# Moving three pieces of work in a two-layer hybrid decoder trunk on one core

## The chip, the core and the metric

The kernel runs on one core of a Trainium2 chip. A core has TensorE (PE; its weight loads are shown as PEld), VectorE (DVE), ScalarE (ACT), GpSimd (POOL) and SyncE (SP, which here only starts transfers). The metric is the device time of one execution in microseconds (us).

## What is computed

The reference is a trunk of two layers over one sequence of 256 tokens with 1024 features, all in float32. Each layer is a feed-forward block, a token mixer and a second feed-forward block; each of the three has its own norm, and a conditioning vector `c` gives every one of them a shift, a scale and a gate by a product with `w_ada`.

```python
for l in range(DEPTH):                                   # 2
    mod = (silu(c) @ w_ada[l] + b_ada[l]).reshape(B, 3, 3, D_MODEL)
    # norm_mod(h, j) = rms(h) * g_norm[l, j] * (1 + mod[:, j, 1]) + mod[:, j, 0];  gate(j) = 1 + mod[:, j, 2]
    x = x + 0.5 * gate(0) * swiglu(norm_mod(x, 0), w_ffn_up[l, 0], w_ffn_down[l, 0])   # hidden width 2816
    x = x + gate(1) * mixer(norm_mod(x, 1), ...)
    x = x + 0.5 * gate(2) * swiglu(norm_mod(x, 2), w_ffn_up[l, 1], w_ffn_down[l, 1])
# mixer: one input projection feeds a gated linear recurrence (512 wide), a stick-breaking attention
# and a forgetting attention (256 each); each result is RMS-normed over its own features, the three are
# concatenated, scaled and multiplied by w_out.
```

## The kernel before

**Precision and weight units.** Every product of a weight runs as three passes (high x high, high x low, low x high), so each operand exists as a high part and a low part. Weights come in units of 128 x 1024 (512 KB). `unit` starts the transfer into one of 6 `raw` buffers (queue of SP), and `split` makes the high part `H` on ACT (line 246) and the low part `L` on DVE (line 247). H and L have 11 buffers each.

**Conditioning dots.** A step of `ada_step` moves one 512 KB unit of `w_ada` through the same `raw` buffers and the same queue of SP and multiplies it with `c` on DVE with an accumulated sum: `ada_ss` (line 292, shift and scale) and `ada_gate` (line 317, gate). 128 steps stand in one list in the order in which the norms and gates need them. `ADA_FFN` and `ADA_MIX` (line 69) say how many are taken off the list after each chunk of a feed-forward block and after each projection of the mixer of a layer; `ada_until` takes what is left when a norm or a residual needs it. In the mixer of layer 0 there are nine projections and ten steps (`proj` takes one each, `proj_w` of the stick-breaking group one for each of its two halves); in layer 1 there are none. After the mixer of layer 0 eleven more are forced by the norm of the next block.

**Feed-forward block.** `ffn` walks 11 chunks of 256 hidden features. The first block of layer 0 has a path of its own (`pre`); the other three take the `else` list of line 568. There `u` (`up`) is the 24 products of one chunk for one half `t` of the tokens (128 tokens), followed by silu on ACT and a multiply on DVE; `r` (`tr`) transposes that product on PE into a PSUM tile `tg` of the pool `PT` and splits it (ACT line 535, DVE line 536); `d` (`down`) is its 12 products with the down weights; `w` (`up_w`) does a half chunk for all tokens, which needs no transposes. The block begins while the norm of the second half of the tokens is still being made: `flush` puts that half's transposes (`norm_out`, tile `tp`, line 418, also pool `PT`, which has two buffers) behind a product inside `u(1, 0)`, and `u(0, 1)` is the first that reads the result (`hTh`, `hTl`).

**Mixer.** The projections come in the order LG, LX (gate and input of the recurrence, one call per half of the tokens, LG 0, LX 0, LG 1, LX 1), FX, SB, VV. As in the feed-forward block, the norm of the second half of the tokens is finished inside LX 0. The recurrence ends in `hs` (scan on DVE, times the transposed gate `tl`). `group` norms a result over its features: a square on ACT, adds on DVE, one product with ones (`mo`, line 801, which sums over partitions), logarithm and exponential on ACT, a multiply on DVE. For `hs` this is written ahead of the VV projections. The attention products that follow are placed with `behind(...)`, an edge that only says after which instruction of the same engine one may be issued.

**Who sets the order.** The code is written in program order, and the framework's planner orders each engine's queue ahead of time: among the instructions whose inputs its own clock takes to be ready, the one written first goes first, and `high_priority` moves an instruction ahead in that choice. On the chip each queue then runs in that fixed order.

Of the kernel before, what the change touches and what calls it, by code (L numbers as in the profile page):

```python
# [9 lines left out]
F32 = mybir.dt.float32  # L10
# [14 lines left out]
SEQ = 256  # L25
# [4 lines left out]
LX, LG, SB, FX, VV = range(5)  # L30
# [14 lines left out]
def weight_units():  # L45
    keys = []
    for l in range(DEPTH):
        for s in range(2):
            for j in range(NCH):
                keys += [("up", l, s, j, h) for h in range(4)] + [("dn", l, s, j, i) for i in range(2)]  # L50
            if s == 0:
                for g in GROUP_ORDER:
                    keys += [("in", l, g, h) for h in range(4)]
                keys += [("out", l, m) for m in range(KT)]
    return {k: i for i, k in enumerate(keys)}
# [10 lines left out]

N_PRE = 4
K_T = (4, 2, 4)
ADA_FFN, ADA_MIX = ((5, 4), (5, 3), (5, 1), (5, 2)), (1, 0)
W_UNITS = weight_units()  # L70
A_UNITS = ada_units()

# [22 lines left out]
def trunk_kernel(ctx: ExitStack, tc: tile.TileContext, x, c, wst, ada, par, cst, row, wg, out):  # L95
# [14 lines left out]
    def W4(shape, dt=F32, name="w4"):  # L110
        return w4.tile(shape, dt, tag="w4", name=name)

    def W2(shape, dt=F32, name="w2"):
        return w2.tile(shape, dt, tag="w2", name=name)
# [4 lines left out]
    def PA(shape, name):  # L119
        return psa.tile(shape, F32, tag="a", name=name)  # L120
# [4 lines left out]
    def PT(shape, name):  # L125
        return pst.tile(shape, F32, tag="t", name=name)

    V, A, T, S = nc.vector, nc.scalar, nc.tensor, nc.sync
# [67 lines left out]
    ones_r, ntri_r, nones_r = (const.tile([128, 128], F32R, name=n + "_r") for n in ("ones", "ntri", "nones"))  # L196
# [53 lines left out]
    def unit(key):  # L250
        if key not in live:
            raw = rawp.tile([128, 1024], F32, tag="raw", name="raw")
            S.dma_start(out=raw, in_=wst[W_UNITS[key]])
            live[key] = split(raw)
        return live[key]
# [6 lines left out]
    def over_features(o, t, w, mid=None, by=4):  # L262

        hh, hl = hT[t]
        muls = []
        for k0 in range(0, KT, by):
            for k in range(k0, k0 + by):
                for i, part in enumerate(w(k)):  # L270
                    T.matmul(o, lhsT=hh[:, k, :], rhs=part, start=k == 0 and i == 0, stop=False)  # L271
            for k in range(k0, k0 + by):
                mul = T.matmul(o, lhsT=hl[:, k, :], rhs=w(k)[0], start=False, stop=k == KT - 1)  # L273
                muls.append(mul)
                if mid and mid[0] == k:
                    mid[1](mul)
        return muls
# [62 lines left out]
    def ada_step(n):  # L340
        for _ in range(n):
            if ada_todo:
                f, a = ada_todo[-1]
                if f is ada_gate and a[2] == 0:
                    if not gate_free[a[1] % 2]:
                        return
                    gate_free[a[1] % 2] = False
                ada_todo.pop()
                f(*a)
# [110 lines left out]
    def act(*a, **k):  # L460
        with tc.issue_after(table[-1].ins) if table else nullcontext():
            used.append(A.activation(*a, **k))  # L462
        return used[-1]
# [9 lines left out]
    def ffn(l, s, after, pre={}):  # L473
# [88 lines left out]
        u, w, r, d = up, up_w, tr, down  # L562
        if pre:
            ops = [(w, (0, 0)), (w, (0, 1)), (w, (1, 0)), (w, (1, 1)), (d, (0, 0)), (w, (2, 0)), (d, (0, 1)),
                   (w, (2, 1)), (d, (1, 0)), (w, (3, 0)), (d, (1, 1)), (w, (3, 1)), (w, (4, 0)), (d, (2, 0)),
                   (d, (2, 1)), (w, (4, 1)), (d, (3, 0)), (d, (3, 1))]
        else:
            ops = [(u, (0, 0)), (u, (1, 0)), (r, (0, 0)), (u, (0, 1)), (r, (1, 0)), (d, (0, 0)), (u, (1, 1)),
                   (r, (0, 1)), (d, (1, 0)), (w, (2, 0)), (r, (1, 1)), (d, (0, 1)), (w, (2, 1)), (d, (1, 1))]
        a, b = NCH - 2, NCH - 1  # L570
        for j in range(5 if pre else 3, a):
# [13 lines left out]
    def mixer(l, after):  # L585
# [7 lines left out]
        muls = {}  # L593

        def proj(g, t):
            o = PA([128, 512], name="pj")

            def w(k):
                q = slice((k % 2) * 512, (k % 2 + 1) * 512)
                return [part[:, q] for part in unit(("in", l, g, k // 2))]  # L600

            muls[g, t] = over_features(o, t, w, (K_T[2], flush) if (g, t) == (LX, 0) else None, by=1)
            ada_step(ADA_MIX[l])
            return o

        def proj_w(g, b):
# [16 lines left out]
        def behind(mul):  # L623
            return tc.issue_after(mul.ins)
# [6 lines left out]
        for t in range(NT):  # L631
            act(lgt[:, t], proj(LG, t), AF.Gelu_apprx_tanh)
            tok = W2([128, 512], name="lxt")
            A.copy(tok, proj(LX, t))
            tp = PT([128, 4, 128], name="tx")
            for i in range(4):
                T.transpose(tp[:, i, :], tok[:, i * 128:(i + 1) * 128], ident)
            A.copy(xT[:, :, 3 + t * 128:3 + (t + 1) * 128], tp)


        u = W4([128, 4, SEQ], name="u")
# [28 lines left out]
        qa = [const.tile([128, 8, 66], F32, name=f"qa{t}", tag=f"qa{t}") for t in range(NT)]  # L670
        for t in range(NT):
            o = proj(FX, t)
            if t == 1:
                z4 = SM([128, NT, 4], name="z4")
# [12 lines left out]
            sq = W2([128, 8, HD], name="fsq")  # L687
# [42 lines left out]
        hs = W4([128, 4, SEQ], name="hs")  # L730
# [45 lines left out]
        def split(f0, n, src):  # L776
            for i in range(n):
                g = gm[:, f0 + i:f0 + i + 1]
                yh, yl = hTh[:, :, f0 + i, :], hTl[:, :, f0 + i, :]
                y = src[:, i, :].rearrange("p (t q) -> p t q", t=NT)  # L780
                A.activation(yh, y, AF.Copy, scale=g)
                V.scalar_tensor_tensor(out=yl, in0=y, scalar=g, in1=yh.bitcast(F32),
                                       op0=ALU.mult, op1=ALU.subtract)
# [6 lines left out]
            q = slice(t * 128, (t + 1) * 128)  # L790
            V.tensor_tensor(out=hs[:, :, q], in0=hs[:, :, q], in1=tp, op=ALU.mult)

        def group(y, n, sq, out):

            A.activation(sq, y, AF.Square)
            while n > 1:
                n //= 2
                V.tensor_tensor(out=sq[:, 0:n, :], in0=sq[:, 0:n, :], in1=sq[:, n:2 * n, :], op=ALU.add)
            n = out.shape[1]
            mo = PT([128, SEQ], name="mo")  # L800
            T.matmul(mo, lhsT=ones_r.bitcast(F32), rhs=sq[:, 0, :], start=True, stop=True)
            rl = W2([128, SEQ], name="rl")
            act(rl, mo, AF.Ln, scale=1.0 / (128 * n), bias=eps_t)
            act(rl, rl, AF.Exp, scale=-0.5)
            V.tensor_tensor(out=out, in0=y, in1=rl.unsqueeze(1).to_broadcast([128, n, SEQ]), op=ALU.mult)

        group(hs, 4, W4([128, 4, SEQ], name="lsq"), hs)

        vt = W4([128, 2, 512], name="vt")
        for t in range(NT):  # L810
            A.copy(vt[:, t], proj(VV, t))
        split(0, 4, hs)


# [64 lines left out]

        def normed(f0, y):  # L880
            yn = W2([128, 2, SEQ], name="yn")
            group(y, 2, W2([128, 2, SEQ], name="gsq"), yn)
            split(f0, 2, yn)

        yfx, ysb = (PD([128, 2, SEQ], name=n) for n in ("yfx", "ysb"))
        values(yfx, 256, lambda part, p, e: (pa, pb)[part][:, 2 * p + e, :])
        normed(6, yfx)
        o = {}

# [20 lines left out]
        for m, t in [(m, 0) for m in WO[:4]] + [(m, 1) for m in WO[:1]] + [(m, 0) for m in WO[4:-2]]:  # L910
            mul = w_out(m, t)
            if (m, t) == (WO[1], 0):
                with behind(mul):
                    values(ysb, 0, lambda part, p, e: (wsa, wsb)[part][:, e, p, :])
                normed(4, ysb)
                load_table("silu_and_others")
# [56 lines left out]
    for l in range(DEPTH):  # L973
        ffn(l, 0, norm(l, 1), pre if l == 0 else {})
        mixer(l, norm(l, 2))
        ffn(l, 1, norm(l + 1, 0) if l + 1 < DEPTH else None)
# [94 lines left out]
```

## Time and profile before

| | |
|---|---|
| time, median of 3 runs | 1011.37 us (1008.23 to 1013.19) |
| profiled execution | 1010.85 us, of which the span from first to last instruction is 1009.0 us |
| PE / PEld / DVE / ACT busy | 982.2 / 857.9 / 761.4 / 532.9 us |
| share of the chain that ended last: PE / DVE / ACT | 86% / 7% / 5% |
| mean granted TensorE clock | 0.995 of full |

All times inside the execution are counted from the start of the span. Matmuls overlap in the profile, so the rate of PE is read from the starts of successive products, and lost time from the gaps between them. In the timeline a bracket at the end of a row is idle time of the engine just before the row and what released it.

### The profile page before, as it was taken

The page shows a single profiled execution, that of the slowest core. Times are in us where ns is not written, and L with a number is a line of the kernel's source. Part 1 is how long each engine was busy: PE and PEld are TensorE (multiplying, and loading weights), DVE is VectorE, ACT ScalarE, POOL GpSimd, SP SyncE. Part 2 cuts the span into 40 slices and gives each one's busy share as a digit, 9 for nine tenths or more (in the row PEclk, how much of TensorE's full clock was granted, in tenths as well). Part 3 has the DMA queues.
Part 4 walks back from the last instruction along what each step waited for, and adds up shares of the span by engine and source line. Part 5 has one row for each costly group of instructions (what it writes and reads, how often), then busy time and mean ns, then how long its engine had stood idle before and what let it go on. Part 6 is the DMA issues. An engine that isn't in the chain of part 4 may idle for free.

```text
span 1009.0 us, 15828 instructions
## 1 busy us (share of the span) xinstructions
PE 982.2 (97%) x6054; PEld 857.9 (85%) x6054; DVE 761.4 (75%) x1224; ACT 532.9 (53%) x854; POOL 6.9 (1%) x16
## 2 busy tenths in 40 slices
PE   6999999989999999999999999999999999999998
PEld 4999999867867799999878999997788778999996
DVE  8988888788996988888589888765778588636352
ACT  5373435558775534355465344455678655535340
POOL 0000000000000000000000000000000000000000
PEclk9999999999999999999999999999999999999999
DMA  8999999677382999999449999854542349655511
GB/s 320 352 336 341 350 330 342 237 259 268 127 279 96 318 370 331 343 327 329 171 165 339 361 346 335 310 177 157 189 167 84 105 155 343 241 180 192 185 64 42
DMA packets 69966, 251.26 MB, mean 249 GB/s; under 512 B 8066, under 2 KB 8706, under 8 KB 69891
## 3 DMA queue, kind: packets, MB, share of 16 engines
q1 hardware_dynamic: 68834, 247.09, 69.3%
q0 software_dynamic: 1056, 3.17, 1.0%
q8 instruction: 47, 0.77, 0.3%
q14 instruction: 29, 0.23, 0.1%
HBM read 249.16 MB, written 1.07 MB: 248 GB/s over the span
## 4 chain that ended last, share of the span: by engine, by line
PE 86%; DVE 7%; ACT 5%; issue 1%; DMA 1%; ACTq 0%; DVEq 0%; SPq 0%
PE up L470 38%; PE dn L258 8%; PE dn L260 8%; PE dn L259 8%; PE up L271 6%; PE pj L271 5%; PE up L273 3%; PE pj L273 2%; DVE L L247 2%; PE wo L258 1%; PE wo L259 1%; PE wo L260 1%; ACT hf L426 1%; ACT H L246 1%; DVE raw L292 1%
## 5 line engine op out<-in xcount | busy, mean ns | idle before, releaser
L247 DVE TENSOR_TENSOR L<-raw,H 128x1024 fp32r<-128x1024 f32 x320 | 381.5, 1220 | 79.1 <-ACT H L246 78.0
L246 ACT CAST H<-raw 128x1024 fp32r<-128x1024 f32 x320 | 327.9, 1051 | 114.1 <-DMA raw<-in_wst 61.3
L470 PE MATMUL up<-hTh,H 128*128 128x256 f32 x1088 | 209.9, 280 | 2.4 <-ACT H L246 1.9
L470 PE MATMUL up<-hTl,H 128*128 128x256 f32 x1088 | 210.0, 281 | 0.0
L470 PE MATMUL up<-hTh,L 128*128 128x256 f32 x1088 | 209.3, 280 | 0.0
L470 PEld LDWEIGHTS up<-hTh,H 128*128 128x128 f32 x1088 | 167.5, 188 | 8.8 <-ACT H L246 2.3
L470 PEld LDWEIGHTS up<-hTl,H 128*128 128x128 f32 x1088 | 163.8, 188 | 0.3 <-DVE hTl L955 0.3
L470 PEld LDWEIGHTS up<-hTh,L 128*128 128x128 f32 x1088 | 163.9, 189 | 0.0
L462 ACT ACTIVATE sg<-up 128x256 f32<-128x256 f32 x88 | 33.8, 384 | 209.5 <-PE up L470 168.1
L258 PE MATMUL dn<-H,gh 128*128 128x512 f32 x352 | 140.4, 399 | 1.3 <-ACT gh L535 1.1
L260 PE MATMUL dn<-H,gl 128*128 128x512 f32 x352 | 139.7, 397 | 0.0
L259 PE MATMUL dn<-L,gh 128*128 128x512 f32 x352 | 139.0, 395 | 0.0
L292 DVE SCALAR_TENSOR_TENSOR raw<-raw,cb 128x1024 f32<-128x1024 f32 x96 | 114.9, 1219 | 1.8 <-DMA raw<-in_ada 1.4
L260 PEld LDWEIGHTS dn<-H,gl 128*128 128x128 f32 x352 | 66.0, 188 | 16.0 <-DVE gl L536 0.9
L258 PEld LDWEIGHTS dn<-H,gh 128*128 128x128 f32 x352 | 66.2, 188 | 14.9 <-ACT gh L535 3.2
L519 DVE TENSOR_TENSOR sg<-sg,up 128x256 f32<-128x256 f32 x68 | 28.5, 419 | 65.6 <-ACT sg L462 65.1
L259 PEld LDWEIGHTS dn<-L,gh 128*128 128x128 f32 x352 | 66.2, 188 | 12.5
L271 PE MATMUL up<-H,hTh 128*128 128x512 f32 x160 | 64.8, 405 | 0.7 <-DVE hTh L431 0.6
L271 PE MATMUL up<-L,hTh 128*128 128x512 f32 x160 | 63.9, 400 | 0.0
L273 PE MATMUL up<-H,hTl 128*128 128x512 f32 x160 | 57.5, 396 | 0.0
L317 DVE SCALAR_TENSOR_TENSOR raw<-raw,cb 128x1024 f32<-128x1024 f32 x48 | 56.8, 1217 | 0.7 <-DMA raw<-in_ada 0.7
L271 PE MATMUL pj<-H,hTh 128*128 128x512 f32 x128 | 52.5, 410 | 1.2 <-DVE hTh L431 1.2
(229 smaller groups left out, 1051.5 us busy)
## 6 DMA issues: line engine op xcount, KB each, us to landing
raw<-in_wst SPq DMA_DIRECT2D x320, 512.0 KB, 5.2
raw<-in_ada SPq DMA_DIRECT2D x144, 512.0 KB, 5.3
gate<-row POOLq DMA_DIRECT2D x6, 512.0 KB, 6.9
x<-in_x SPq DMA_DIRECT2D x2, 512.0 KB, 4.3
wgt<-in_wg SPq DMA_DIRECT2D x2, 512.0 KB, 6.6
out_x<-x SPq DMA_DIRECT2D x4, 256.0 KB, 2.0
once<-in_cst SPq DMA_DIRECT2D x1, 192.0 KB, 5.4
p_sb<-in_par SPq DMA_DIRECT2D x1, 168.0 KB, 5.2
```

What stands on the lines that cost most here:

```text
L246: A.copy(h, raw)
L247: V.tensor_tensor(out=lo, in0=raw, in1=h.bitcast(F32), op=ALU.subtract)
L258: T.matmul(o, lhsT=xh, rhs=wh, start=first, stop=False)
L259: T.matmul(o, lhsT=xh, rhs=wl, start=False, stop=False)
L260: return T.matmul(o, lhsT=xl, rhs=wh, start=False, stop=last)
L271: T.matmul(o, lhsT=hh[:, k, :], rhs=part, start=k == 0 and i == 0, stop=False)
L273: mul = T.matmul(o, lhsT=hl[:, k, :], rhs=w(k)[0], start=False, stop=k == KT - 1)
L292: V.scalar_tensor_tensor(out=raw, in0=raw, scalar=1.0, in1=cb, op0=ALU.mult, op1=ALU.mult, accum_out=st[:, v, k:k + 1])
L317: V.scalar_tensor_tensor(out=raw, in0=raw, scalar=1.0, in1=cb, op0=ALU.mult, op1=ALU.mult, accum_out=col[:, k:k + 1])
L462: used.append(A.activation(*a, **k))
L470: return T.matmul(o[:, v], lhsT=w[:, q:q + 128], rhs=(hTh, hTl)[h][:, :, k, :], start=opens, stop=True, skip_group_check=True)
L519: V.tensor_tensor(out=sg, in0=sg, in1=o[:, 1], op=ALU.mult)
```

## The change

It has three parts. In the `else` list of `ffn`, the transposes `r(0, 0)` are written ahead of `u(1, 0)`, and `d(0, 0)` directly behind `u(1, 0)`, ahead of `u(0, 1)`; nothing else in the list moves. In the mixer `group` is cut in two: the squares and adds (`squares`) stay where they were, while the product `mo` and what follows are written behind the VV projections, with the product alone given priority and allowed from the fifth feature block of VV 0 on (`muls[VV, 0][4]`, the 15th of its 24 products). The conditioning steps of the mixer of layer 0 are taken only at FX, VV (two for each call) and SB (two for each half): none at LG and LX, four at FX, four at SB, four at VV, twelve instead of ten in all, so nine are left to be forced.

```diff
-ADA_FFN, ADA_MIX = ((5, 4), (5, 3), (5, 1), (5, 2)), (1, 0)
+ADA_FFN, ADA_MIX = ((5, 4), (5, 3), (5, 1), (5, 2)), (2, 0)
@@ ffn
-            ops = [(u, (0, 0)), (u, (1, 0)), (r, (0, 0)), (u, (0, 1)), (r, (1, 0)), (d, (0, 0)), (u, (1, 1)),
+            ops = [(u, (0, 0)), (r, (0, 0)), (u, (1, 0)), (d, (0, 0)), (u, (0, 1)), (r, (1, 0)), (u, (1, 1)),
                    (r, (0, 1)), (d, (1, 0)), (w, (2, 0)), (r, (1, 1)), (d, (0, 1)), (w, (2, 1)), (d, (1, 1))]
@@ mixer, proj
-            ada_step(ADA_MIX[l])
+            ada_step(ADA_MIX[l] if g in (FX, VV) else 0)
@@ mixer, norm of a group
-        def group(y, n, sq, out):
+        def squares(y, n, sq):
 
             A.activation(sq, y, AF.Square)
             while n > 1:
                 n //= 2
                 V.tensor_tensor(out=sq[:, 0:n, :], in0=sq[:, 0:n, :], in1=sq[:, n:2 * n, :], op=ALU.add)
+            return sq[:, 0, :]
+
+        def group(y, sq, out, at=None):
+
             n = out.shape[1]
             mo = PT([128, SEQ], name="mo")
-            T.matmul(mo, lhsT=ones_r.bitcast(F32), rhs=sq[:, 0, :], start=True, stop=True)
+            with ExitStack() as place:
+                if at:
+                    place.enter_context(tc.high_priority())
+                    place.enter_context(behind(at))
+                T.matmul(mo, lhsT=ones_r.bitcast(F32), rhs=sq, start=True, stop=True)
             rl = W2([128, SEQ], name="rl")
...
-        group(hs, 4, W4([128, 4, SEQ], name="lsq"), hs)
+        lsq = squares(hs, 4, W4([128, 4, SEQ], name="lsq"))
 
         vt = W4([128, 2, 512], name="vt")
         for t in range(NT):
             A.copy(vt[:, t], proj(VV, t))
+        group(hs, lsq, hs, muls[VV, 0][4])
         split(0, 4, hs)
...
-            group(y, 2, W2([128, 2, SEQ], name="gsq"), yn)
+            group(y, squares(y, 2, W2([128, 2, SEQ], name="gsq")), yn)
```

## Rows read from the trace of the kernel before

**Rows 1.** The page: busy time, share of span, instructions of each engine.
```profile
PE 982.2 (97%) x6054; PEld 857.9 (85%) x6054; DVE 761.4 (75%) x1224; ACT 532.9 (53%) x854; POOL 6.9 (1%) x16
```

**Rows 2.** Timeline of PE, layer 0: start, duration, instruction, [idle before].
```profile
194.43 0.40 PE L271 MATMUL up<-H,hTh 128*128 128x512 f32 x1
...
207.96 0.50 PE L271 MATMUL pj<-H,hTh 128*128 128x512 f32 x1 [1.24 <-DVE hTh L431]
...
223.39 1.12 PE L637 MATMUL tx<-c_sb,lxt 128*128 128x128 f32 x4 [1.69 <-ACT lxt L634]
...
224.73 0.63 PE L271 MATMUL pj<-L,hTh 128*128 128x512 f32 x1
...
241.91 1.12 PE L662 MATMUL go<-u,wgt 128*128 128x256 f32 x4
```

**Rows 3.** Timeline of PE, the same first and last place in layer 1.
```profile
691.68 0.39 PE L271 MATMUL up<-H,hTh 128*128 128x512 f32 x1
...
734.79 1.12 PE L662 MATMUL go<-u,wgt 128*128 128x256 f32 x4
```

**Rows 4.** DVE by line, 205 to 220 us: count, busy us, mean ns.
```profile
L317 DVE SCALAR_TENSOR_TENSOR raw<-raw,cb 128x1024 f32<-128x1024 f32 x2 | 2.4, 1212 | 0.0
...
L292 DVE SCALAR_TENSOR_TENSOR raw<-raw,cb 128x1024 f32<-128x1024 f32 x1 | 1.2, 1218 | 0.0
```

**Rows 5.** Stretches: length, busy PE, PEld, DVE, ACT, POOL, granted clock, DMA share.
```profile
223.11:226.52 3.41, 3.13 (x10) 2.65 (x11) 2.66 (x4) 1.34 (x3) 0.54 (x1) 0.50 0.46 183
...
827.27:830.68 3.41, 3.41 (x8) 2.73 (x9) 3.41 (x7) 1.56 (x2) 0.00 (x0) 0.50 0.76 300
...
242.00:280.00 38.00, 35.82 (x240) 30.10 (x240) 33.54 (x62) 28.79 (x67) 0.00 (x0) 1.00 0.48 162
280.00:300.00 20.00, 20.00 (x107) 14.23 (x106) 19.06 (x36) 16.86 (x36) 0.00 (x0) 1.00 0.85 274
```

**Rows 6.** Timeline of PE around the norm product, layer 0 and layer 1.
```profile
277.00 0.40 PE L273 MATMUL pj<-H,hTl 128*128 128x512 f32 x1
277.23 0.39 PE L271 MATMUL pj<-H,hTh 128*128 128x512 f32 x1
279.49 0.67 PE L801 MATMUL mo<-lsq,ones_r 128*128 128x256 f32 x2 [1.86 <-DVE lsq L798]
...
769.92 0.40 PE L271 MATMUL pj<-L,hTh 128*128 128x512 f32 x1
771.09 0.67 PE L801 MATMUL mo<-lsq,ones_r 128*128 128x256 f32 x2 [0.77 <-DVE lsq L798]
```

**Rows 7.** Timeline of PE in the three feed-forward openings.
```profile
333.44 1.27 PE L418 MATMUL tp<-c_sb,xn 128*128 128x128 f32 x8
335.75 0.44 PE L532 MATMUL tg<-c_sb,sg 128*128 128x128 f32 x2 [1.04 <-ACT hf L426]
...
336.99 0.39 PE L271 MATMUL up<-H,hTh 128*128 128x512 f32 x1
...
524.72 0.60 PE L418 MATMUL tp<-c_sb,xn 128*128 128x128 f32 x4
...
526.87 0.47 PE L271 MATMUL up<-H,hTh 128*128 128x512 f32 x1
...
824.04 1.27 PE L418 MATMUL tp<-c_sb,xn 128*128 128x128 f32 x8
...
827.85 0.63 PE L271 MATMUL up<-H,hTh 128*128 128x512 f32 x1
```

**Rows 8.** Timelines of ACT and DVE: the first chunk's silu and multiply.
```profile
327.78 0.38 ACT L462 ACTIVATE sg<-up 128x256 f32<-128x256 f32 x1
...
328.20 0.42 DVE L495 TENSOR_TENSOR sg<-sg,up 128x256 f32<-128x256 f32 x1
```

**Rows 9.** The page, costliest groups: mean ns; idle before.
```profile
L247 DVE TENSOR_TENSOR L<-raw,H 128x1024 fp32r<-128x1024 f32 x320 | 381.5, 1220 | 79.1 <-ACT H L246 78.0
```

**Rows 10.** Who waited for whom: total us, times, longest us.
```profile
ACT H L246 <- DMA raw<-in_wst: 61.3, 40, 6.2
```

## The prediction

> **What bounds the kernel now.** I read the page first: PE is busy for 97% of the span [rows 1], and the chain that ended last is mostly PE. So only time in which PE stands or runs slowly can be won. I then went through the starts of successive PE instructions. In the long middle of each feed-forward block they follow each other without a gap, so nothing is to be had there. What PE loses lies in a few places, and all three edits aim at such places: the passage from the first block of layer 0 into its mixer [rows 2], the wait for the norm product [rows 6], and the openings of the three other feed-forward blocks [rows 7]. At two of them PE also falls to half clock: the granted clock is 0.50 (1.2 GHz) at 223.11 to 226.52 and at 827.27 to 830.68 [rows 5], each time just after PE had stood for the norm of the second half of the tokens [rows 2, 7]. A product of 512 columns follows the last one after 0.23 us at full clock [rows 6].
>
> **Part 1, conditioning dots out of the first projections (layer 0).** Layer 1 runs the same mixer code with no dots, so it is the row for what the change leaves. From the last up products of the block to the first gate product `go`, layer 0 takes 241.91 - 194.43 = 47.48 us and layer 1 takes 734.79 - 691.68 = 43.11 us: 4.37 us apart [rows 2, 3]. The difference has a visible cause. Between 205 and 220 us DVE runs three dots of 1.21 us each [rows 4], between the steps of the reciprocal root that the norm of the second half waits for; PE waits for its transposes, then 1.69 us more in front of `tx`, and runs at half clock after it [rows 2, 5]. After the change no dot is written before FX, its transfer stands behind four FX units in SP's queue, and it can hardly land before that chain is over. I take 4.0 us of the 4.37, with 2.0 and 4.4 as ends, since the first four dots will still land while LG 1 and LX 1 run.
>
> The dots don't vanish. Twenty of them run in layer 0 after 194 us; seven of these run before `go`, where I expect about three, so some four move behind it, in front of VV's products and the attention. There DVE is busy for 33.54 of 38 us and then for 19.06 of 20 us [rows 5]. Layer 0 needs 279.49 - 241.91 = 37.58 us from `go` to `mo` and layer 1 needs 36.30 us [rows 2, 3, 6], with four dots in this stretch against none: 0.32 us of path for one dot. Four more cost 1.3 us. The ends are 0 (free slots in DVE) and 4.9 us (four at their full 1.21 us each). SP's queue is the same length in all; the units of SB and VV come behind four more transfers each, but are needed many products later. The five of them that make the gate also release POOL's two transfers of it later; gate, shift and scale are needed only after the output projection. Part 1 is worth 4.0 - 1.3 = **2.7 us**.
>
> **Part 2, the norm product later.** `mo` sits behind the 10th VV product in layer 0 and behind the 11th in layer 1. PE starts it 279.49 - 277.23 = 2.26 us after the product ahead of it, and 1.17 us in layer 1 [rows 6]; without the 0.23 us of that product itself the waits are 2.03 and 0.94 us, for the last add of `lsq` on DVE. The products behind `mo` have their operands and stand only because PE takes its queue in order. Put behind the 15th product, `mo` has 5 x 0.23 = 1.15 us more cover in layer 0 and 4 x 0.23 = 0.92 us in layer 1. So 1.15 + 0.92 = **2.1 us**, with about 0.9 us of the wait left in layer 0. The ends are 0 (the adds come later too, because more dots stand ahead of them) and 3.0 us (both waits go). The logarithm, exponential and multiply follow as late as `mo`, but `wo` reads their result many products later.
>
> **Part 3, the openings.** `tg` must wait for one of the two `PT` buffers that the norm's `tp` has just taken, until ACT has read it (1.04 us in the bracket); then the down product waits for the split of `tg`, and `u(0, 1)` for the norm [rows 7]. With `r(0, 0)` done inside `u(1, 0)` the buffers are free, and twelve down products (12 x 0.23 = 2.8 us) lie ready to run while ACT and DVE finish the norm. From the first `tp` to the first product of `u(0, 1)` the stretch is 336.99 - 333.44 = 3.55, 526.87 - 524.72 = 2.15 and 827.85 - 824.04 = 3.81 us. The work in it, at full rate, is eight `tp` (about 1.1 us; four, 0.36 us, in the second), two `tg` (0.14) and in the first and third one down product (0.23). What PE loses is 2.1, 1.65 and 2.3 us. In the third, the eight products in the half-clock stretch took 3.41 us instead of 8 x 0.23 = 1.84; I count 1.2 us of this, as the slow stretch starts with a wait. Together 7.3 us.
>
> Against this stands a new wait. `r(0, 0)` needs silu and multiply of `u(0, 0)` at once: silu starts at 327.78 and the multiply ends at 328.62 [rows 8], 0.84 us later; before, a whole chunk lay in between. The planner can put some products of `u(1, 0)` in front of the transposes; I take 0.4 us for each opening, with ends of 0 and 1.0. The split `gl` also enters DVE's queue ahead of chunk 1's low parts (1.22 us each [rows 9]) and of the norm, which moves them by about 0.4 us; they are ready shortly ahead of use, and the 12 down products cover the norm. The transfers keep their order, and the down units stand split by then already. Part 3 is 7.3 - 3 x 0.4 = **6.1 us**, ends 0 (below) and 7.3.
>
> **Sum.** 2.7 + 2.1 + 6.1 = 10.9 us off the profiled execution's 1010.85 us gives 1000.0 us. That execution lies 0.5 us under the median of 1011.37, so I let both stand for the same.
>
> **Rivals.**
> *The transposes gain nothing* (0.16). Order on PE is the planner's. If it leaves `tg` behind `tp` as now, or if the wait for the product eats what is won, part 3 is 0: 1010.85 - 4.8 = 1006.0. For it: silu and multiply stand in crowded queues. Against it: with 24 products of `u(1, 0)` to put in front, a planner has room.
>
> *The dots block DVE* (0.14). The moved dots fall into the chain of recurrence, `lsq` and attention, in the stretches where DVE is 88 and 95% busy [rows 5]. If four run at full price, part 1 is 4.0 - 4.9 = -0.9 and part 2 is 0, since the adds are late: 1010.85 - 6.1 + 0.9 = 1005.7; if dots also stand between the projections' steps, so that part 1 wins only 2.0, 1007.7. For it: 1.1 us of the 1.28 us by which layer 0 is behind is the wait for `lsq`.
>
> *Slower: PE stands for a transfer* (0.08). In the openings silu stands in ACT's queue behind casts of weight units. A cast that waits for its unit holds ACT up: 40 such waits, the longest 6.2 us [rows 10]. Until now the 24 products of `u(1, 0)` (5.5 us) lay in front of the transposes; now PE stands at `r(0, 0)` for as long as ACT does, and everything behind it too. At 6.2 us in each of the three openings the time is 1010.85 - 4.8 - 7.3 + 18.6 = 1017.4. It decides from a wait of (4.8 + 7.3) / 3 = 4.0 us on. Against it: at 327.78 silu follows a cast that did not wait [rows 8]. The Trainium skill, "TensorE: Matmul & The Clock Gate", the table at its head, gives ScalarE and VectorE a strict first-in, first-out queue, and its Part 3 (Packing small matmuls) has matmuls start in order, while weight loads may be pulled ahead. The trace agrees as far as it goes: the products behind `mo` stood for 2.03 us [rows 6]. By that rule a late silu reaches PE in full, which is a reason against putting `r(0, 0)` early; it gives this rival its price.
>
> **Chances and range.** The forecast has 0.60, the three rivals 0.16, 0.14 and 0.08, something not seen 0.02. If every upper end holds, 4.4 + 3.0 + 7.3 = 14.7 us go: 996. Low ends in two parts, or one of the first two rivals, give 1006 to 1008. So 996 to 1008.5; the slower rival stays outside. A measurement of this kernel tells about 0.5% (5 us) from no change, so "faster" ends at 1006.3. The forecast and half of the first two rivals lie below it: 0.60 + 0.15 = 0.75. Their other half and half of what is not seen give same 0.16, the slower rival and the rest 0.09.
>
> **What would show it.** In the changed trace: no L317 or L292 in DVE between 205 and 220 us; `tp` in layer 0 without its long wait and no half clock near 223; the stretch to `go` near 43.5 us in both layers; `mo` behind five or four more products with a wait under 1 us; in the openings `tg` inside `u(1, 0)` and twelve down products in a row behind `tp`, with no half clock at 827. Wrong would be: a gap of PE in front of the early `tg` of over 1 us, low parts of chunk 1 late behind `gl`, `go` to `mo` in layer 0 over 39 us, or a half-clock stretch in a new place, which costs about 1.5 us each.

## The result, and the profile after

| | before | after |
|---|---|---|
| time, median | 1011.37 us | 1003.77 us (5 runs, 1003.41 to 1003.98) |
| ratio after / before, 95% interval | | 0.9926 (0.9914 to 0.9937) |
| profiled execution / its span | 1010.85 / 1009.0 us | 1003.98 / 1001.8 us |

The forecast was 1000.0 us with a range of 996 to 1008.5. The time lies inside and on the side that was given 0.75, but 3.8 us above the forecast, and one of the three parts went the other way. So the first thing to read is not the total but a ledger by place: the starts of the same PE instructions in both traces, and the time between them. Page of the changed kernel, engines and the shares of the chain that ended last:

```profile
PE 978.9 (98%) x6054; PEld 857.9 (86%) x6054; DVE 761.7 (76%) x1224; ACT 531.9 (53%) x854; POOL 6.9 (1%) x16
...
PE 91%; DVE 4%; ACT 2%; DMA 1%; issue 1%; ACTq 0%; DVEq 0%
```

PE lost 3.3 us of its busy time against [rows 1]; its own work is the same. The chain holds more PE and less DVE and ACT. Timeline of PE in the changed kernel, layer 0, then the opening of the next feed-forward block (start, duration, instruction, idle before and its releaser):

```profile
194.25 0.40 PE L271 MATMUL up<-H,hTh 128*128 128x512 f32 x1
...
207.03 0.40 PE L271 MATMUL pj<-H,hTh 128*128 128x512 f32 x1
...
218.82 1.27 PE L418 MATMUL tp<-c_sb,xn 128*128 128x128 f32 x8 [0.43 <-ACT xn L407]
...
222.10 1.11 PE L637 MATMUL tx<-c_sb,lxt 128*128 128x128 f32 x4 [2.00 <-ACT lxt L634]
...
241.90 0.48 PE L662 MATMUL go<-u,wgt 128*128 128x256 f32 x1 [0.63 <-DVE u L655]
...
281.94 0.39 PE L273 MATMUL pj<-H,hTl 128*128 128x512 f32 x1
283.80 0.67 PE L809 MATMUL mo<-lsq,ones_r 128*128 128x256 f32 x2 [1.48 <-DVE lsq L798]
...
321.18 0.49 PE L418 MATMUL tp<-c_sb,xn 128*128 128x128 f32 x3
...
350.53 0.38 PE L532 MATMUL tg<-c_sb,sg 128*128 128x128 f32 x2
```

From rows like these, with [rows 2, 3, 6] and the same two last instructions in the trace of before (319.15 and 350.96 us), comes the ledger. Layer 1 runs from 691.68 to 809.76 us before and from 689.72 to 806.63 us after; the second and third opening run from 509.43 to 541.16 and from 809.76 to 843.11 us before, from 509.01 to 539.19 and from 806.63 to 835.95 us after. The stretches lie end to end; "opening" runs from the first half's `tp` of a feed-forward block to the `tg` of `r(0, 1)`.

| stretch | before | after | difference |
|---|---|---|---|
| layer 0, last up products to first projection (LG 0) | 13.53 | 12.78 | -0.75 |
| layer 0, LG 0 to `go` | 33.95 | 34.87 | +0.92 |
| layer 0, `go` to `mo` | 37.58 | 41.90 | +4.32 |
| layer 0, `mo` to `tp` of the next block | 39.66 | 37.38 | -2.28 |
| layer 1, last up products to `tp` of the next block | 118.08 | 116.91 | -1.17 |
| the three openings | 31.80 + 31.72 + 33.34 | 29.34 + 30.18 + 29.31 | -8.03 |
| sum | | | -6.99 |

The profiled execution got 6.87 us shorter and its span 7.2 us, of which 0.18 us lies ahead of the first stretch (194.43 against 194.25 us); so next to nothing is left over. The openings gave more than was forecast, the norm product gave something in layer 1, and layer 0's mixer, where the dots were moved, got 2.2 us **longer**.

One caution belongs to the third and fourth row. `mo` is not at the same place in PE's queue: between `go` and `mo` there are 37 products of 512 columns in the trace of before and 45 after, and behind `mo` 11 fewer: it stands behind the 21st product of VV 0, not behind the 15th, from which on it is allowed (in layer 1 it is the 15th). A product costs 0.23 us [rows 6], so 1.9 us of the 4.32 only moved across the boundary and come back in the next row. Likewise 120 products instead of 117 stand between LG 0 and `go`, 0.7 us. What holds without such a correction is the sum over layer 0: +2.21 us.

The three openings in PE's timeline read alike, and the list of waits has one of PE in each of the first and third, 0.3 us for the first half's `hTh`, which before has too; the last one:

```profile
816.45 0.39 PE L271 MATMUL up<-H,hTh 128*128 128x512 f32 x1
816.68 0.38 PE L532 MATMUL tg<-c_sb,sg 128*128 128x128 f32 x2
816.82 0.48 PE L271 MATMUL up<-L,hTh 128*128 128x512 f32 x1
...
820.64 0.60 PE L418 MATMUL tp<-c_sb,xn 128*128 128x128 f32 x4
820.99 0.48 PE L271 MATMUL up<-L,hTh 128*128 128x512 f32 x1
821.31 0.60 PE L418 MATMUL tp<-c_sb,xn 128*128 128x128 f32 x4
821.66 0.48 PE L273 MATMUL up<-H,hTl 128*128 128x512 f32 x1
821.97 0.39 PE L259 MATMUL dn<-L,gh 128*128 128x512 f32 x1
...
824.30 0.39 PE L260 MATMUL dn<-H,gl 128*128 128x512 f32 x1
824.53 0.40 PE L271 MATMUL up<-H,hTh 128*128 128x512 f32 x1
```

No row has a bracket. `tg` stands among the products of `u(1, 0)`, the `tp` come in two fours between products (in the second opening in one eight), and from 821.97 to 824.30 eleven down products run one after the other while ACT and DVE finish the norm. Compare [rows 7], where the same work took 3.81 us from `tp` to the first product of `u(0, 1)` with PE mostly standing or at half clock.

DVE in the norm of layer 0's second half shows what went wrong (timeline of DVE, changed kernel), and SP shows why (timeline of SP; a row of several transfers lasts from the first issue to the last, pauses included):

```profile
215.21 0.21 DVE L364 TENSOR_SCALAR ny<-na,ny 128x1 f32<-128x1 f32 x1
215.33 1.22 DVE L317 SCALAR_TENSOR_TENSOR raw<-raw,cb 128x1024 f32<-128x1024 f32 x1
...
216.66 1.22 DVE L317 SCALAR_TENSOR_TENSOR raw<-raw,cb 128x1024 f32<-128x1024 f32 x1
...
217.80 0.21 DVE L364 TENSOR_SCALAR ny<-na,ny 128x1 f32<-128x1 f32 x1
217.93 1.22 DVE L317 SCALAR_TENSOR_TENSOR raw<-raw,cb 128x1024 f32<-128x1024 f32 x1
...
219.07 1.23 DVE L317 SCALAR_TENSOR_TENSOR raw<-raw,cb 128x1024 f32<-128x1024 f32 x1
...
220.23 0.40 DVE L428 TENSOR_SCALAR hf<-tp,G,S 128x128 f32<-128x128 f32 x1
```

```profile
184.79 16.02 SPq L253 DMA_DIRECT2D raw<-in_wst  x5
203.44 10.93 SPq L315 DMA_DIRECT2D raw<-in_ada  x4
215.36 1.56 SPq L253 DMA_DIRECT2D raw<-in_wst  x2
```

The dots written behind FX sit in the very chain that they were to leave: two between the steps of the root (`ny`), two between the root and the first use of `tp` (L428). That is four, where three stood before [rows 4]. Their transfers were issued at 203.44, 211.64, 212.85 and 214.04 us and landed at 207.03, 215.14, 217.43 and 218.66 us, each ahead of its dot. The four units ahead of them, FX's, had gone out between 185.93 and 200.49 us, when the first projection began only at 207.03 us. SP's waits for these four are for DVE to be done with `raw` buffers (12.0 us in all, the longest 7.8 us, for `L` of line 247): SP runs ahead of the products as far as these buffers come free.

Windows of the changed kernel (length, busy PE, PEld, DVE, ACT, POOL, granted clock, DMA share, GB/s) answer to [rows 5]:

```profile
221.30:224.50 3.20, 2.40 (x8) 2.11 (x9) 2.04 (x4) 1.96 (x4) 0.00 (x0) 0.52 1.02 417
...
242.00:280.00 38.00, 35.43 (x235) 30.07 (x236) 34.90 (x64) 29.01 (x69) 0.00 (x0) 1.00 0.65 212
280.00:300.00 20.00, 18.52 (x93) 13.42 (x92) 19.84 (x35) 15.13 (x34) 0.00 (x0) 1.00 0.74 236
```

Near 222 us PE runs at the 1.2 GHz level as before (clock 0.52 over that window; 0.50 from 221.43 to 224.85 us): the clock falls inside the 2.00 us wait in front of `tx`. DVE has become fuller, 34.90 instead of 33.54 of the 38 us, and PE emptier. At 827 us there is no half-clock stretch any more.

### The profile page after: what moved, and what is told of

It reads as the page before. It is cut to its first block, busy times and chain, and to the rows that moved or that the text cites. A ratio compares the mean times of both kernels' runs of the same rounds, so it can differ in the third digit from the quotient of the medians.

```text
span 1001.8 us, 15817 instructions
## 1 busy us (share of the span) xinstructions
PE 978.9 (98%) x6054; PEld 857.9 (86%) x6054; DVE 761.7 (76%) x1224; ACT 531.9 (53%) x854; POOL 6.9 (1%) x16
## 4 chain that ended last, share of the span: by engine, by line
PE 91%; DVE 4%; ACT 2%; DMA 1%; issue 1%; ACTq 0%; DVEq 0%
PE up L470 39%; PE dn L258 8%; PE dn L260 8%; PE dn L259 8%; PE up L271 8%; PE up L273 4%; PE pj L271 4%; PE pj L616 2%; PE pj L273 2%; PE wo L258 1%; PE wo L259 1%; PE wo L260 1%; DVE L L247 1%; DMA raw<-in_wst 1%; PE tp L418 1%
```

## The experiments

Two theories stood against each other. The **placement theory**: a dot costs PE by where it stands in DVE's queue; the four at FX still stand in the norm, and more of them now stand between `go` and `mo`. Its rival, the **transfer theory**: what costs are the dots' transfers, which push weight units back in SP's queue. Beside that, each part had to be measured alone.

### The parts alone

`a_only` is the kernel before with part 3 alone, `b_only` with part 2 alone, `c_only` with part 1 alone, `ab` with parts 2 and 3. The edits are those lines of the change; for `c_only`:

```diff
-ADA_FFN, ADA_MIX = ((5, 4), (5, 3), (5, 1), (5, 2)), (1, 0)
+ADA_FFN, ADA_MIX = ((5, 4), (5, 3), (5, 1), (5, 2)), (2, 0)
-            ada_step(ADA_MIX[l])
+            ada_step(ADA_MIX[l] if g in (FX, VV) else 0)
```

Expected of `a_only`:

> Only the new order of the feed-forward openings; mixer and dots as before. Theory (each part acts in its own place; from the two traces the three openings give about 1.6, 2.5 and 4.0 us): 8 us under the kernel before, 1002.5 to 1004. Rival (part of what the openings seem to gain was won by the mixers' later or earlier ends in front of them): 5 us or less under it, over 1006.

Expected of `b_only`:

> Only the norm product later (both layers). Theory (the changed kernel's mixer of layer 0 lost its time to the dots): 1.0 to 1.3 us less in each layer from the first gate product to the end of the projections, in all 2.0 to 2.6 us under the kernel before, and the wait for lsq in layer 0 falls from 1.9 to about 0.8 us. Rival (the later place itself costs in layer 0, as PE waited 1.5 us at it there in the changed kernel): no gain in layer 0, in all at most 1.2 us.

Expected of `c_only`:

> Only the conditioning dots moved. Theory (four dots still land inside the norm of the second half of the tokens, and the others crowd the stage from the gate products to the norm product): slower than before by 2.5 to 4 us, with the stretch from the last up products to the gate products no shorter than 47 us in layer 0. Rival (the dots are harmless, part 2 or 3 hurts the mixer of layer 0): 1 us under the kernel before or better, that stretch near 44 us.

Expected of `ab`:

> New openings and later norm product, dots where they were. Theory: the sum of the two, about 10.5 us under the kernel before and 2.5 to 3.5 us under the changed kernel: 1000 to 1001.5. Rival (the dots' move gains and the rest loses): slower than the changed kernel, over 1004.

Measured (before in the same call: 1011.54 us):

| kernel | median us | ratio, 95% interval | layer 0 | layer 1 | openings | half clock in PE |
|---|---|---|---|---|---|---|
| before | 1011.37 | | 124.72 | 118.08 | 31.80, 31.72, 33.34 | 223, 827 us |
| after | 1003.77 | 0.9926 (0.9914 to 0.9937) | 126.93 | 116.91 | 29.34, 30.18, 29.31 | 221 us |
| a_only | 1002.73 | 0.9915 (0.9900 to 0.9930) | 124.22 | 118.05 | 29.31, 30.16, 29.33 | none |
| b_only | 1006.85 | 0.9959 (0.9943 to 0.9975) | 123.05 | 116.90 | 31.80, 31.72, 31.80 | none |
| c_only | 1012.51 | 1.0011 (0.9998 to 1.0023) | 127.00 | 118.12 | 33.35, 31.73, 31.80 | 223, 339 us |
| ab | 1000.33 | 0.9888 (0.9872 to 0.9905) | 124.57 | 116.92 | 29.32, 30.17, 29.32 | 224 us |

"Layer 0" and "layer 1" are the stretch from the last up products to `tp`. (All of these also have a short half-clock stretch at their end, and before one near 18 us.) What follows:

- **Part 3** saves 2.5, 1.55 and 2.5 us wherever it is in, beside the 1.54 us by which the last opening is longer when it holds a half-clock stretch (33.34 against 31.80 in `b_only`, with the same waits).
- **Part 1** costs 2.28 us of layer 0 alone (`c_only` against before) and 2.36 us on top of the others (after against `ab`); all four have a half-clock stretch near 223 us. By the ratios it costs 3.8 us on top of the others (0.9926 against 0.9888) and 1.1 us alone, with an interval that touches no change.
- **Part 2** saves 1.18 us in layer 1. In layer 0 it saves 1.1 us from `go` on by itself and 0.9 us beside part 3 (`ab` against `a_only`); beside part 1 it saves nothing there: 126.93 us with it, 127.00 without. In `c_only`, which has no part 2, the order of PE's queue has put `mo` just as late, behind the 21st product of VV 0, and it stands just as long, so part 2 had nothing left to move:

```profile
284.34 0.45 PE L801 MATMUL mo<-lsq,ones_r 128*128 128x256 f32 x1 [1.43 <-DVE lsq L798]
```

`a_only` and `ab` came out where the theory had them. `c_only` lost 1.0 us in the medians where 2.5 to 4 was expected, though its 47.60 us from the up products to `go` are as expected. `b_only` gained 4.7 us where 2.0 to 2.6 was expected; the two stretches that part 2 acts on gave 2.25 us of it, and most of the rest lies where before's trace has a half-clock stretch and `b_only`'s has none (1.54 us in the last opening, 0.78 us from LG 0 to `go`).

### Which of the two moves works in part 3

`a_r` moves only `r(0, 0)` ahead of `u(1, 0)`, `a_d` only `d(0, 0)` ahead of `u(0, 1)`:

```diff
-            ops = [(u, (0, 0)), (u, (1, 0)), (r, (0, 0)), (u, (0, 1)), (r, (1, 0)), (d, (0, 0)), (u, (1, 1)),
# a_r
+            ops = [(u, (0, 0)), (r, (0, 0)), (u, (1, 0)), (u, (0, 1)), (r, (1, 0)), (d, (0, 0)), (u, (1, 1)),
# a_d
+            ops = [(u, (0, 0)), (u, (1, 0)), (r, (0, 0)), (d, (0, 0)), (u, (0, 1)), (r, (1, 0)), (u, (1, 1)),
```

Expected of `a_r`:

> Of the openings only the transposes r(0, 0) are written ahead of u(1, 0); d(0, 0) stays behind u(0, 1). An opening from its first tp to the transposes of the second half's first chunk took 31.80, 31.72 and 31.80 us without half clock, and 29.3, 30.2 and 29.3 us with both moves. Theory (the transposes' wait for a PT buffer is the cost, and the planner fills the norm's wait with down products once their input is there): 29.3 to 30.3 us. Rival (the down products' own place matters): 31 us or more.

Expected of `a_d`:

> Of the openings only the down products d(0, 0) are written ahead of u(0, 1); r(0, 0) stays behind u(1, 0). Theory: the transposes still wait about 1.0 us for a PT buffer and the down products 0.5 us for their split, so 31 us or more in the first and third opening. Rival: 30 us or less.

Measured, one execution each, before beside them 1013.59 us: `a_r` 1003.97 us with openings of 29.39, 30.48 and 29.41 us; `a_d` 1010.83 us with 31.81, 31.87 and 33.28 us. The early transposes bring nearly all, the early down products nothing by themselves. The reason is in `a_d`'s timeline of PE:

```profile
333.30 1.27 PE L418 MATMUL tp<-c_sb,xn 128*128 128x128 f32 x8
335.61 0.44 PE L532 MATMUL tg<-c_sb,sg 128*128 128x128 f32 x2 [1.04 <-ACT hf L426]
336.50 0.50 PE L258 MATMUL dn<-H,gh 128*128 128x512 f32 x1 [0.46 <-ACT gh L535]
```

`tg` still stands behind `tp` for a `PT` buffer, and the down products still stand behind `tg`. Once `tg` is early the down products are ready, and the order of the queue puts them into the norm's gap without being told.

### Taking the four dots out of the norm

`after_hold` is the changed kernel with one edge more: the dots of FX may be issued on DVE only behind the last subtraction of the second half's norm.

```diff
             last_v = V.tensor_tensor(out=hl[:, r4, :], ...)
         if t == 0:
             norm_end.update(A=last, V=last_v)
+        else:
+            norm_end.update(V1=last_v)
...
-            ada_step(ADA_MIX[l] if g in (FX, VV) else 0)
+            with tc.issue_after(norm_end["V1"].ins) if g == FX else nullcontext():
+                ada_step(ADA_MIX[l] if g in (FX, VV) else 0)
```

> The changed kernel, with the four FX dots held in DVE's queue behind the last step of the norm of the second half of the tokens (nothing else moves). Theory (these four dots, at 215.3 to 220.2 us of the changed kernel, are why the first stretch did not shorten): the stretch from LG 0 to go in layer 0 falls from 34.9 to 31 to 32 us, with no half clock there, and the kernel is 2 to 4 us under the changed one; go to mo stays near 42 us. Rival (the norm's chain is late for another reason, the splits of the weights or the residual): the stretch stays over 34 us.

Measured: 1002.33 us, ratio 0.9898 (0.9879 to 0.9916), before beside it 1011.59 us. That is 1.4 us under the changed kernel, where 2 to 4 was expected. Timeline of DVE: the dots now start behind the norm's last `hTl`.

```profile
219.93 0.42 DVE L431 CAST hTh<-hf 128x512 fp32r<-128x512 f32 x1
220.38 1.29 DVE L434 TENSOR_TENSOR hTl<-hf,hTh 128x512 fp32r<-128x512 f32 x2
221.60 1.22 DVE L317 SCALAR_TENSOR_TENSOR raw<-raw,cb 128x1024 f32<-128x1024 f32 x1
```

LG 0 to `go` falls from 34.87 to 30.05 us (layer 1: 30.34); 0.7 us of this are the three products, which stand behind `go` again. From the last up products to `go` it is 12.78 + 30.05 = 42.83 us, 4.65 us under before. So the four dots' place in DVE's queue was the whole difference there. The Trainium skill, "TensorE: Matmul & The Clock Gate", the table at its head, calls the queues of ScalarE and VectorE strictly first-in, first-out; the trace agrees, since an order among DVE's instructions alone gave some 4 us on PE. But `go` to `mo` became 44.32 us (48 products instead of 45 in front of `mo`, so 0.7 us of it moved over), and a half-clock stretch stands at 259 us. The sum of layer 0 is 124.99 us: of the 4.8 us, 1.9 us stay.

### Doing no dots at all

In `after_light` and `ab_light` the transfers stay as they are in the changed kernel and in `ab`, and each of the 21 dots of layer 0's mixer and of the norm behind it is replaced by a copy of one column (shown for the gate; the dots of shift and scale likewise):

```diff
-        V.scalar_tensor_tensor(out=raw, in0=raw, scalar=1.0, in1=cb, op0=ALU.mult, op1=ALU.mult,
-                               accum_out=col[:, k:k + 1])
+        V.tensor_copy(col[:, k:k + 1], raw[:, 0:1])
```

Expected of `after_light`:

> The changed kernel with the DVE work of the 21 dots of the mixer of layer 0 left out (one column is copied instead of the product and sum over 1024); their transfers stay, in the same places of SP's queue. Theory (DVE is what the moved dots cost): layer 0 comes near layer 1, LG 0 to go 30 to 31 us and go to mo 36 to 37 us. Rival (the dots' transfers, which now stand in front of the units of SB and VV, are the cost): go to mo stays at 39 us or over.

Expected of `ab_light`:

> As the run before, on the kernel with the other two parts alone (dots where they were, their DVE work left out, transfers kept). Both: LG 0 to go 30 to 31 us, go to mo 36 to 37 us. It is the floor against which the run before is read: if the transfers' new place costs anything, that one is slower than this one by it.

Measured, one execution each: 996.44 and 997.05 us; layer 0 takes 119.16 and 119.83 us. Inside the layer the two don't split as expected (LG 0 to `go` 29.40 and 31.77 us, `go` to `mo` 38.35 and 36.05 us), with 114 and 119 products ahead of `go`. With the same transfers, the loss of part 1 is gone, and the two orders are alike. The transfer theory falls: the 2.3 us are DVE's work. (A copied dot also frees its `raw` buffer about 1 us earlier, which these runs don't separate; `after_hold`, which keeps the buffers of four dots longer, was faster up to `go` all the same.) In all, the 21 dots cost 126.93 - 119.16 = 7.8 us in the changed kernel and 124.57 - 119.83 = 4.7 us in `ab`; both figures contain the half-clock stretch near 223 us, which the light kernels don't have.

### Holding the next group too

`after_hold_sb` adds to `after_hold` that the SB dots wait on DVE for the last copy of FX's feature preparation (line 718):

```diff
-            V.tensor_scalar(out=qa[t][:, 4:8, 65:66], in0=ft, scalar1=-1.0, scalar2=None, op0=ALU.mult)
+            qa_end = V.tensor_scalar(out=qa[t][:, 4:8, 65:66], in0=ft, scalar1=-1.0, scalar2=None, op0=ALU.mult)
...
-            ada_step(ADA_MIX[l])
+            with tc.issue_after(qa_end.ins):
+                ada_step(ADA_MIX[l])
```

> The changed kernel with the FX dots held behind the norm, as in the earlier run, and the four SB dots held behind the last copy of the forget gate sums into the keys (DVE, end of the FX stage). Theory (four dots in a row in front of FX's second half are what go to mo pays for: 44.3 us there with FX held, 41.9 in the changed kernel): 41 us or less from go to mo, and no wait of zo or fp over 0.5 us. Rival (the number of dots ahead of mo is the cost, wherever they stand): 43 us or more.

Measured, one execution: 1002.22 us. `go` to `mo` fell to 40.55 us, as expected, though with 51 products in front of `mo`. But `mo` to `tp` grew from 37.84 to 40.51 us, since the dots that are due before the next block's norm now crowd in front of it. Waits of PE, 194 to 325 us (total, times, longest):

```profile
PE tp L418 <- ACT xn L407: 3.0, 2, 2.5
PE mo L813 <- DVE lsq L802: 1.7, 1, 1.7
PE up L271 <- DVE hTh L431: 1.5, 1, 1.5
```

and the first opening went back to 31.68 us, with the granted clock at 0.50 from 318 to 324.8 us. Layer 0 takes 123.24 us, 1.75 less than `after_hold`; the opening gives 2.3 us back. Postponing the same number of dots only moves where they are paid.

### One dot for each projection, held behind the norm

`ab_hold` takes `ab` (one dot for each projection, as before the change), leaves the dot at LG 0 away, and holds those of LX 0, LG 1, LX 1 and FX behind the second half's norm:

```diff
-            ada_step(ADA_MIX[l])
+            with tc.issue_after(norm_end["V1"].ins) if g in (LG, LX, FX) and (g, t) != (LG, 0) else nullcontext():
+                ada_step(0 if (g, t) == (LG, 0) else ADA_MIX[l])
```

> New openings and later norm product, dots one per call as before, but none at LG 0, and those of LX 0 to FX 1 held behind the same step of the norm. Theory: LG 0 to go falls to 31 to 32 us (from 35.0 in the run with both other parts) and go to mo stays at 37 to 39 us, so 3 us under that run: 997 to 998.5, the fastest of all. Rival (held dots keep the raw buffers of the weights, so that FX and SB come late): no gain, 1000 or over, and go to mo over 40 us.

Measured: **996.68 us, ratio 0.9844 (0.9827 to 0.9860)**, before beside it 1011.59 us: faster than both kernels. Layer 0 takes 119.69 us, the same as `ab_light`, which does no dots there at all: all 21 dots run, and none is paid for. They don't run singly: the five held ones start at 223.32, 224.46, 225.61, 227.89 and 229.03 us, close together right behind the norm, and LG 0 to `go` takes 30.20 us, as in layer 1 (30.33). PE in `ab_hold`, layer 0:

```profile
207.96 0.40 PE L271 MATMUL pj<-H,hTh 128*128 128x512 f32 x1
...
238.16 1.13 PE L665 MATMUL go<-u,wgt 128*128 128x256 f32 x4
...
277.45 0.67 PE L812 MATMUL mo<-lsq,ones_r 128*128 128x256 f32 x2 [1.39 <-DVE lsq L801]
...
314.86 0.66 PE L418 MATMUL tp<-c_sb,xn 128*128 128x128 f32 x4
```

How the dots lie, counted by their starts in DVE's timeline:

| kernel | LG 0 to `go` | of these inside the norm | `go` to `mo` | `mo` to `tp` | layer 0, us |
|---|---|---|---|---|---|
| before | 5 | 3 | 4 | 9 | 124.72 |
| after | 8 | 4 | 7 | 6 | 126.93 |
| after_hold | 6 | 0 | 7 | 8 | 124.99 |
| after_hold_sb | 4 | 0 | 8 | 9 | 123.24 |
| ab_hold | 6 | 0 | 4 | 11 | 119.69 |

(before has two more ahead of LG 0, and one more dot in the stretch near 189 us.) The kernel that is best has none in the norm, few between `go` and `mo`, and most behind `mo`. That is read off five kernels; the places behind `go` were not tested one by one.

## Why the prediction was right or wrong

The forecast was 10.9 us from parts 1, 2 and 3 as 2.7 + 2.1 + 6.1. The ledger and the single runs give -2.3, about +1.3 and +8.0: 7.0 us. That the total still lies in the range is luck in part: part 1 came out 5.0 us under its forecast, near the worst that the prediction gave it (2.0 - 4.9 = -2.9), and the openings made up for 1.9 us of this by giving more than their upper end of 7.3.

**Part 1, first step: wrong.** It failed at "its transfer stands behind four FX units in SP's queue, and it can hardly land before that chain is over". Two things were not read. The first is how far SP runs ahead: FX's units were issued from 185.93 us on and the dots' own from 203.44 us on, and all four had landed by 218.66 us, 4.4 us ahead of the norm's last step (`hTl`, at 223.04). The second is that landing alone does not decide. The order of DVE's queue is fixed beforehand, and it had the dots between the steps of the root whatever the transfers did. The diagnosis ahead of that step was right: layer 0 was behind layer 1 because of dots in the norm, and taking them out for good (`after_hold`) gives 4.65 us from the up products to `go`, above the 4.0 taken and the 4.4 given as the end. (One reading was loose: of the three dots in [rows 4] two stand between the steps of the root, at 216.61 and 217.95 us; the one at 211.14 us stands ahead of its first step at 215.23 us.) Of the changed kernel's own two terms, 0.75 us came before LG 0 and -0.92 us behind it, so this step brought -0.2 us in place of 4.0 (+0.5 if the three products more in front of `go` are taken out).

**Part 1, second step: the mechanism right, count and price too low.** Some four dots were to move behind `go`; 13 stood there before and 13 after. What changed was their place: seven instead of four between `go` and `mo`, four of them close together (starts from 249.86 to 254.57 us, 1.21 to 1.22 us each). From `go` to `tp` layer 0 lost 2.04 us in place of 1.3 (2.7 with those three products); against `ab`, which has part 2 as well, it is 3.2 us. `go` to `mo` over 39 us, listed as a sign of being wrong, came: 41.90 us. The waits of PE in the changed kernel, 194 to 321 us, beside the one for `lsq` of [rows 6]:

```profile
PE pj L271 <- ACT qkT L771: 1.6, 1, 1.6
PE mo L809 <- DVE lsq L798: 1.5, 1, 1.5
PE zo L683 <- ACT zs L680: 1.0, 1, 1.0
...
PE go L662 <- DVE u L655: 0.6, 1, 0.6
```

In `after_light`, with the same transfers and without the dots' work, those for `qkT` and `u` are gone, and `zo` stands 0.4 us. The price of 0.32 us for a dot was an average over dots that stand apart. In `ab_hold` such dots are free; in the changed kernel 21 dots cost 7.8 us. There is no one price for a dot.

**Part 2: right alone, half of it lost beside part 1.** By itself it gives 1.18 + 1.1 = 2.3 us where 2.1 was forecast, in layer 1 with the wait for `lsq` gone (`mo` at 769.15, 0.45 us after the product ahead of it instead of 1.17 [rows 6]). Beside part 1 layer 0's share is nil: the low end that the prediction named, "the adds come later too, because more dots stand ahead of them". The planner had put `mo` behind the 21st product there with or without part 2, so the 15th place that the sum was made for never came about. The two parts were costed as if they were independent; they share DVE.

**Part 3: right, a little too small.** The early `tg` meets no wait, so the reserve of 3 x 0.4 us for silu and multiply was not needed: products of `u(1, 0)` stand in front of it, as the prediction thought possible. Without it the forecast would have been 7.3 us; 8.03 came, of which 1.54 us is the half-clock stretch at 827 us where 1.2 was counted. The remaining 0.4 us is spread over the first and third opening (the second gave 0.1 us less than counted) and was not traced further. That the early transposes work and the early down products alone do not (`a_r`, `a_d`) bears out the step: `tg`'s place in the `PT` buffers was what held the opening up.

**The rivals.** That the transposes gain nothing did not happen, nor the slower one: no opening has a wait of PE at its transposes or behind the norm. "The dots block DVE" is what happened to part 1, in both places that it named, and partly to part 2. Its time of 1005.7 us is nearer to the measured 1003.77 us than the forecast of 1000.0. It had 0.14. For a step that moves work into a queue which is 88% and 95% busy [rows 5], that was too little.

**What would show it.** Of the signs listed, those of part 3 came true, and the wait of `mo` went in layer 1 alone. Those of part 1 all failed: dots at 215 to 220 us, half clock near 222 us, 47.65 us from the up products to `go` instead of 43.5.

**What stays open.** `after_hold` and `ab_hold` both keep the norm free, and yet layer 0 differs by 5.3 us. `after_hold` has a half-clock stretch at 259 us, and waits of 1.5 us for `qkT` and 1.3 us for `lf` which `ab_hold` has not; it also takes two dots for a call instead of one, and three more before `mo`. Which of these comes first was not separated.

## What to carry to other kernels

A filler instruction is not placed by the line at which it is written: look where it ends up in its engine's queue, and if it must stay out of a chain, tie it behind that chain's last instruction. Put such fillers where the engine they run on has nobody waiting: at such a place five in a row cost nothing here, while dots that were only postponed were paid at the next chain. A transpose that shares two buffers with a chain's own belongs ahead of that chain, and then the products behind it fill the chain's gap.

## What the runs showed that was not expected

**Half-clock stretches come and go with the same waits ahead of them.** Before and `b_only` have the same waits in the last opening (1.04 us at `tg`, 0.46 us at the down product); before falls to a granted clock of 0.50 at 827 us, `b_only` stays at 1.00. `c_only` has its own at 339 us instead. In an opening one costs 1.54 to 1.55 us (33.34 against 31.80, 33.35 against 31.80). In layer 0's passage the traces give no one price: LG 0 to `go` is 33.95 us (before) and 34.98 us (`ab`) with it, 33.69 us (`a_only`, where PE stands 0.58 us for DVE in front of `go`) and 33.18 us (`b_only`) without. This bears on why the parts' medians don't add up: 8.8 us (`a_only`) and 4.7 us (`b_only`) against 11.2 us for both (`ab`). In the profiled executions both half-clock stretches of before are missing in either single run and can be saved only once, and `ab` has one near 224 us again, where LG 0 to `go` is 34.98 us against 33.69 in `a_only`. Executions of one kernel differ in this too: the 13 of before beside these runs had mean granted clocks from 0.991 (1014.42 us) to 0.998 (1009.84 us). One trace for each kernel is one draw, so that part 3 took away the stretch at 827 us, 1.54 us of its 8.03, is likely but not shown: of the four traces without the early transposes three have such a stretch in an opening (before, `a_d`, `c_only`), of those with them only `after_hold_sb`, behind its wait for `xn`.

**All 21 dots fit at no cost.** `ab_hold` does 21 x 1.22 = 25.6 us more of DVE's work between 223 us and the next block than `ab_light`, and layer 0 takes 119.69 against 119.83 us.
